# The last stage of a decode step by token tiles, with the residual turned in 32x32 blocks

## The chip, the cores and the metric

One core of a Trainium2 chip runs the whole program in one launch. The metric is the device time of an execution in microseconds. TensorE (PE) multiplies, VectorE (DVE), ScalarE (ACT) and GpSimd (POOL) work elementwise, and SyncE (SP) issues nearly all DMA transfers, in the order of its own queue.

## The reference

A decoder layer for 1024 prompt tokens and 32 sample tokens of width 1024 (1056 rows in all). Two token mixers, retention and latent attention, work on the same normalised input; their outputs are merged, projected and added to the input. The last stage, which the change touches, is

```python
x = x + merged @ w_out
x = x + sigmoid(x @ w_ple_gate) * (ple @ w_ple_proj)
y = rmsnorm(x, final_norm_w)
```

`w_out` and `w_ple_gate` are 1024x1024, `w_ple_proj` is 256x1024, and `ple` has 256 columns per token. The outputs of the stage are `y_prompt` (1024 rows) and `y_sample` (32 rows).

## The kernel before

Products are made from float32 values in two parts: `hi`, a copy in the type that TensorE multiplies at full rate, and `lo`, the rest. `mac` (L262) makes one product from three matmuls, hi by hi, hi by lo and lo by hi (L266 to L268). `gemm` (L270) keeps 128 output features in the partitions and the tokens in the columns, in three thirds of `TH` = 352 columns; for each third it adds up `nk` blocks of 128 in a bank of PSUM (`mm`, two banks) and calls an eviction. `load_w` (L253) brings a strip of 128 weight columns in two loads (`stage`, L240, with `wr` tiles of 256 KB from SP, two rooms), ScalarE copies `hi`, VectorE subtracts `lo`.

The `w_out` stage (L1549 to L1570) runs over eight strips f. Its eviction adds the transposed input `xT` on VectorE, copies `hi` on ScalarE and subtracts `lo` on VectorE: the new residual stands transposed, features in the partitions, as eight pairs `x1h`, `x1l`. In its course the projection's weights (`wph`, `wpl`) and the first third of the embedding (`pT`) are loaded and split.

The gate stage is `third(j, pT)` (L1573), three times. For each strip f it loads 128 columns of `w_ple_gate` (anew in each third), multiplies projection (`pp`, 2 blocks) and gate (`pg`, 8 blocks) with features in the partitions, and then adds `x1h` and `x1l` to `xr` on GpSimd (L1614), takes the sigmoid on ScalarE (L1617), and product and sum on VectorE (L1618, L1619). After every second strip, `turn` (L1581) turns the strips before back to tokens: six transposes on TensorE (L1588, with the identity), squares with their sums on ScalarE (L1590), and the product with the norm's weights on VectorE (L1596). Behind the fourth turn of a third come the root on GpSimd (L1595), the scaling on ScalarE and VectorE (L1627, L1628) and the output.

Rooms in SBUF are shared by tags: `xs_` has 23 rooms of 4.2 KB per partition, of which `merged` holds 16 until `w_out` is done, `w4` three, `xr_` 17. Which instruction comes next on each engine isn't written out by hand in this stage: the framework puts them in an order when it builds the program, and waits follow from the tiles that are read and written. Earlier in the program `turn_blocks` (L329) already writes tokens as features to DRAM by VectorE's 32x32 transposes and DMAs of 32-element pieces, for the latents (`latD`) and the embedding (`pTD`, L333).

Of the kernel before, what the change touches and what calls it, by code (L numbers as in the profile page):

```python
# [20 lines left out]
P = 128  # L21
# [135 lines left out]
def run(g):  # L157
    for _ in g:
        pass
# [3 lines left out]
def decode_step(ctx: ExitStack, tc: tile.TileContext, A: dict, O: dict):  # L163
# [35 lines left out]
    def lo_of(out, src, hi):  # L199
        dve.tensor_tensor(out=out, in0=src, in1=b32(hi), op=ALU.subtract)  # L200
# [20 lines left out]
    latD = dram.tile([NLAT // 32, 32, SEQ], F32, tag="latD", name="latD")  # L221
    xTD = dram.tile([P, 8, NT], F32, tag="xTD", name="xTD")
    pTD = dram.tile([PLE // 32, 32, NT], F32, tag="pTD", name="pTD")

    w_in = A["w_in"][0]

# [26 lines left out]
    def load_w(src, nk):  # L253

        hi, lo = wtiles()
        src = src.rearrange("(k p) f -> p k f", p=P)
        for k in range(0, nk, 4):
            ks = slice(k, min(k + 4, nk))
            stage(src[:, ks], hi[:, ks], lo[:, ks])
        return hi, lo  # L260
# [923 lines left out]
    def split(raw, hi, lo):  # L1184
        act.copy(hi, raw)  # L1185
        lo_of(lo, raw, hi)
        return hi, lo
# [342 lines left out]
        gx = nxt  # L1530


    def by_tile(j):

        for a in range(0, TH, P):
            b = min(a + P, TH)
            yield a, b, min(b, SEQ - j * TH) - a

    def embedding(j):
        pT = [xs_("pT", (P, 2, TH)) for _ in range(2)]  # L1540
        for k in range(2):
            hi, lo = (pT[k][:, i, :] for i in range(2))
            raw = xs_("pTr", (P, TH), F32)
            sp.dma_start(raw, pTD[4 * k:4 * k + 4, :, j * TH:(j + 1) * TH].rearrange("b i t -> (b i) t"))
            split(raw, hi, lo)
        return pT

    x1, wp = [], []
    for f in range(8):  # L1549
        fs = slice(f * P, (f + 1) * P)  # L1550
        xT = nxt_xT
        w = load_w(A["w_out"][0, :, fs], 8)
        hi, lo = xr_("x1h"), xr_("x1l")
        x1.append((hi, lo))

        def evac(j, ps, sl, hi=hi, lo=lo, xT=xT):
            t = wst.tile([P, TH], F32, tag="gev", name="x1", bufs=2)
            dve.tensor_tensor(out=t, in0=ps, in1=xT[:, sl], op=ALU.add)
            act.copy(hi[:, sl], t)
            lo_of(lo[:, sl], t, hi[:, sl])  # L1560
        if f < 7:
            nxt_xT = x_transposed(f + 1)
        run(gemm(w, merged, evac, 8))
        if f in (3, 4):
            k = f - 3
            wp.append(tuple(xs_(n_, (P, D)) for n_ in ("wph", "wpl")))
            for c in (slice(0, 512), slice(512, D)):
                stage(A["w_ple_proj"][0, k * P:(k + 1) * P, c], wp[k][0][:, c], wp[k][1][:, c])
        if f == 6:
            pT = embedding(0)  # L1570


    def third(j, pT):  # L1573
        sl = slice(j * TH, (j + 1) * TH)
        tiles = list(by_tile(j))
        Y = [xs_("yn", (P, D), F32) for _ in tiles]
        ss = small(pz, "ss", 12, 2)
        pool.memset(ss, 1.0)
        r = small(pz, "r", 3, 2)

        def turn(yT, quarter):  # L1581

            hs = slice(quarter * 256, (quarter + 1) * 256)
            for i, ((a, b, _), yn) in enumerate(zip(tiles, Y)):
                n = b - a
                px = tr()
                for c in range(2):
                    pe.transpose(px[:n, c * P:(c + 1) * P], yT[:, c, a:b], ident)  # L1588
                q = xs_("sq", (P, 256), F32)
                act.activation(q[:n], px[:n, :256], AF.Square, accum_out=ss[:n, 4 * i + quarter:4 * i + quarter + 1])  # L1590
                if quarter == 3:
                    v, of = (small(pz, name, 4 if name == "of" else 1, 2) for name in ("v", "of"))
                    dve.tensor_tensor_reduce(out=of, in0=ss[:, 4 * i:4 * i + 4], in1=fours, scale=1.0 / D, scalar=EPS,
                                             op0=ALU.mult, op1=ALU.add, accum_out=v)
                    pool.tensor_tensor(out=r[:, i:i + 1], in0=v, in1=nhalf, op=ALU.pow)  # L1595
                dve.tensor_tensor(out=yn[:n, hs], in0=px[:n, :256], in1=fnw[:n, hs], op=ALU.mult)  # L1596

        due = None
        for f in range(8):
            fs = slice(f * P, (f + 1) * P)  # L1600
            if f % 2 == 0:
                yT = xs_("yT", (P, 2, TH), F32)
            w = load_w(A["w_ple_gate"][0, :, fs], 8)
            pp = ac()
            for k in range(2):
                mac(pp[:, :TH], tuple(v[:, fs] for v in wp[k]), (pT[k][:, 0, :], pT[k][:, 1, :]), k == 0, k == 1)
            pg = mm()
            for k in range(8):
                mac(pg[:, :TH], (w[0][:, k, :], w[1][:, k, :]), (x1[k][0][:, sl], x1[k][1][:, sl]), k == 0, k == 7)
            if f % 2 == 0 and f:  # L1610
                turn(due, f // 2 - 1)
            y = yT[:, f % 2, :]
            xr = xs_("xr", (P, TH), F32)
            pool.tensor_tensor(out=xr, in0=b32(x1[f][0][:, sl]), in1=b32(x1[f][1][:, sl]), op=ALU.add)  # L1614
            sg = wst.tile([P, TH], F32, tag="gev", name="sg", bufs=2)
            for a, b in [(a, b) for a, b, _ in tiles] if f == 7 and j == 2 else [(0, TH)]:
                act.activation(sg[:, a:b], pg[:, a:b], AF.Sigmoid)  # L1617
                dve.tensor_tensor(out=sg[:, a:b], in0=sg[:, a:b], in1=pp[:, a:b], op=ALU.mult)  # L1618
                dve.tensor_tensor(out=y[:, a:b], in0=sg[:, a:b], in1=xr[:, a:b], op=ALU.add)  # L1619
            due = yT  # L1620
            yield
        turn(due, 3)
        for i in range(3):
            (a, b, m), yn = tiles[i], Y[i]
            n = b - a
            o = xs_("o", (P, D), F32)
            act.activation(o[:n, :448], yn[:n, :448], AF.Copy, scale=r[:n, i:i + 1])  # L1627
            dve.tensor_scalar(o[:n, 448:], yn[:n, 448:], r[:n, i:i + 1], None, op0=ALU.mult)  # L1628
            t0 = j * TH + a
            sp.dma_start(O["y_prompt"][0, t0:t0 + m, :], o[:m])  # L1630
            if m < n:
                sp.dma_start(O["y_sample"].rearrange("b t d -> (b t) d"), o[m:n])

    fours = pz.tile([P, 4], F32, name="fours")
    pool.memset(fours, 1.0)
    fnw = w4("fnw", (P, D), F32)
    sp.dma_start(fnw, A["final_norm_w"].unsqueeze(0).to_broadcast([P, D]))
    last = iter(())
    for j in range(3):
        u = third(j, pT)  # L1640
        next(u)
        run(last)
        for f in range(7):
            next(u)
            if f == 4 and j < 2:
                pT = embedding(j + 1)
        last = u
    run(last)
    rph.close()
    ph.close()  # L1650

# [32 lines left out]
```

## Time and profile before

| | |
|---|---|
| median of 3 runs | 2132.06 us (2128.3 to 2132.3) |
| the profiled execution's own time | 2129.97 us |
| its span | 2128.2 us |
| PE busy | 2091.2 us, 98% |
| DVE busy | 1261.7 us, 59% |
| ACT busy | 723.2 us, 34% |
| POOL busy | 333.1 us, 16% |
| DMA over the span | 316.31 MB, 149 GB/s |

The span runs from the first to the last instruction of the program in the profile; 1.8 us of the execution lie around it. Matmuls overlap each other in the records, so the step from one start to the next tells more than the length of one.

### The profile page before, as it was taken

To read this page: it belongs to the slowest core of one execution; us is meant where nothing else is said; L and a number is where in the kernel's file an instruction comes from. 1 tells how busy PE (TensorE), PEld (TensorE's weight loads), DVE (VectorE), ACT (ScalarE), POOL (GpSimd) and SP (SyncE) were. 2 spreads that over 40 slices of the span, in tenths; PEclk is the share of its full clock that TensorE was granted. 3 is DMA by queue.
4 is the path that set the end of the run, shared out by engine and by line. 5 is a ranking of instruction groups with operands and counts; after the bars stand their busy time and mean duration, and the time that the engine had idled before them with its cause. 6 is when DMAs were issued, how large, how long until landed. Compare 5 with 4: busy or idle time off the path is not lost. (4 is left out here: it accounts for less than half of the span.)

```text
span 2128.2 us, 38977 instructions
## 1 busy us (share of the span) xinstructions
PE 2091.2 (98%) x15408; PEld 1835.8 (86%) x15408; DVE 1261.7 (59%) x2850; ACT 723.2 (34%) x1543; POOL 333.1 (16%) x527
## 2 busy tenths in 40 slices
PE   8999999999999999999999999999999999999998
PEld 7998787787877998888888887888888999999997
DVE  6524556565565357677677764877776353444465
ACT  6312232342423322222222212454565341322343
POOL 2220111111110022222222220122211000000122
PEclk9999999999999999999999999999999999999999
DMA  7576666566564322745626647210112452333243
GB/s 208 133 245 212 236 212 225 219 219 239 201 231 169 121 66 75 240 126 152 209 73 195 177 159 242 48 43 23 35 55 89 140 192 82 100 90 119 84 143 118
DMA packets 330552, 316.31 MB, mean 149 GB/s; under 512 B 92160, under 2 KB 283840, under 8 KB 326272
## 3 DMA queue, kind: packets, MB, share of 16 engines
q1 hardware_dynamic: 303872, 208.28, 33.2%
q0 software_dynamic: 9216, 83.89, 10.6%
q10 hardware_dynamic: 17280, 21.63, 2.8%
q8 instruction: 121, 1.98, 0.4%
q14 instruction: 63, 0.52, 0.1%
HBM read 245.38 MB, written 68.36 MB: 147 GB/s over the span
## 5 line engine op out<-in xcount | busy, mean ns | idle before, releaser
L266 PE MATMUL mm<-xh,wh 128*128 128x352 f32 x1344 | 456.5, 340 | 2.1 <-POOL wh L197 1.6
L268 PE MATMUL mm<-xh,wl 128*128 128x352 f32 x1344 | 436.4, 325 | 2.1 <-DVE wl L200 2.1
L267 PE MATMUL mm<-xl,wh 128*128 128x352 f32 x1344 | 436.5, 325 | 0.0
L266 PEld LDWEIGHTS mm<-xh,wh 128*128 128x128 f32 x1344 | 253.1, 188 | 85.7 <-issue 74.7
L268 PEld LDWEIGHTS mm<-xh,wl 128*128 128x128 f32 x1344 | 254.1, 189 | 4.0 <-DVE wl L200 2.4
L267 PEld LDWEIGHTS mm<-xl,wh 128*128 128x128 f32 x1344 | 254.2, 189 | 3.2 <-issue 2.1
L200 DVE TENSOR_TENSOR wl<-wr,wh 128x512 fp32r<-128x512 f32 (+2 forms) x251 | 176.0, 714 | 128.2 <-ACT wh L247 92.2
L247 ACT CAST wh<-wr 128x512 fp32r<-128x512 f32 x214 | 128.4, 618 | 279.0 <-PE mm L267 247.3
L687 DVE STREAM_TRANSPOSE kt<-craw 128x512 f32<-128x512 f32 x256 | 161.1, 681 | 86.9 <-PE sc L691 80.6
L439 ACT ACTIVATE gev<-mm 128x352 f32<-128x352 f32 x120 | 55.5, 463 | 242.1 <-PE mm L268 230.7
L266 PE MATMUL mm<-mh,wh 128*128 128x352 f32 x384 | 124.5, 324 | 1.4 <-ACT mh L1185 0.8
L267 PE MATMUL mm<-ml,wh 128*128 128x352 f32 x384 | 124.8, 325 | 0.8 <-DVE ml L200 0.6
L268 PE MATMUL mm<-mh,wl 128*128 128x352 f32 x384 | 124.3, 324 | 0.0
L268 PE MATMUL mm<-gh,wl 128*128 128x352 f32 x384 | 124.3, 324 | 0.0
L266 PE MATMUL mm<-gh,wh 128*128 128x352 f32 x384 | 124.3, 324 | 0.0
L267 PE MATMUL mm<-gl,wh 128*128 128x352 f32 x384 | 124.1, 323 | 0.0
L266 PE MATMUL mm<-wv,xh 128*128 128x512 f32 x256 | 103.6, 405 | 0.0
L267 PE MATMUL mm<-wv,xh 128*128 128x512 f32 x256 | 100.9, 394 | 0.0
L268 PE MATMUL mm<-wv,xl 128*128 128x512 f32 x256 | 100.8, 394 | 0.0
L691 PE MATMUL sc<-kt,q 32*32 32x512 f32 x2560 | 91.7, 600 | 0.0
L1614 POOL TENSOR_TENSOR xr<-x1h,x1l 128x352 f32<-128x352 f32 x24 | 26.6, 1131 | 389.0 <-DVE pT L200 311.0
L890 ACT ACTIVATE on<-ac,gb,gs 128x512 f32<-128x512 f32 x36 | 28.0, 778 | 157.9 <-DVE gb L888 152.8
(395 smaller groups left out, 4512.2 us busy)
## 6 DMA issues: line engine op xcount, KB each, us to landing
wr<-in_w_in_dram SPq DMA_DIRECT2D x144, 256.0 KB, 3.8
st<-in_state_ret_dram SPq DMA_DIRECT2D x32, 512.0 KB, 4.7
out_ret_sample_dram<-st SPq DMA_DIRECT2D x32, 512.0 KB, 3.6
wr<-in_w_ple_gate_dram SPq DMA_DIRECT2D x48, 256.0 KB, 2.8
gt<-gev ACTq DMA_DIRECT2D x48, 176.0 KB, 3.7
gl<-go SPq DMA_DIRECT2D x16, 528.0 KB, 5.6
gate<-ga SPq DMA_DIRECT2D x16, 528.0 KB, 3.6
g<-gt SPq DMA_DIRECT2D x32, 256.0 KB, 3.2
```

The source lines that it names most:

```text
L200: dve.tensor_tensor(out=out, in0=src, in1=b32(hi), op=ALU.subtract)
L247: hi_by[0](hi, raw)
L266: pe.matmul(out, wh, xh, start=first, stop=False)
L267: pe.matmul(out, wh, xl, start=False, stop=False)
L268: pe.matmul(out, wl, xh, start=False, stop=last)
L439: act.activation(t, ps, func)
L687: dve.transpose(kt[:, 2 * i + s].rearrange("p (n r) -> p n r", r=32), src)
L691: pe.matmul(sc[32 * v:32 * v + 32, q, :], Q["q4"][qs_, j + v // 2, 2 * (g % 2) + v % 2, :], kt[qs_, v, :], start=n == 0, stop=n == NJ // 2 ...
L890: act.activation(on[:n], po, AF.Identity, bias=nb[:n], scale=s[:n])
L1614: pool.tensor_tensor(out=xr, in0=b32(x1[f][0][:, sl]), in1=b32(x1[f][1][:, sl]), op=ALU.add)
```

## The change

The residual is turned to tokens as soon as it is made. Each eviction of `w_out` also transposes its 128x352 piece in 32x32 blocks on VectorE and writes it with four DMAs of 128-byte pieces to a DRAM tensor `x1D` with one row per token. From there `residual(T)` reads 128 tokens at a time.

Gate and projection products come out by tokens: the tokens' `x1h`, `x1l` (or the embedding's parts) are the stationary side and 512 columns of weights, a half H of the features, the moving one. The weights of a half are loaded and split once, 12 tiles of `xs_` and the `wh`, `wl` rooms; half 0 during `w_out`, half 1 during the first four token tiles. The order of the work is token tiles 0 to 3 in half 0, the same in half 1, then both halves of tiles 4 to 7; the last unit comes in two column halves. `joined` takes sigmoid, product, sum and square by tokens, `normed` the root and the scaling.

The 32 sample tokens leave these products. They are computed in plain float32 from unsplit weights (loaded once more, in 20 pieces of 256 KB), with the 32 tokens as the stationary side and four groups of 128 weight columns side by side in the array's column groups, two pieces behind each unit. A small product with a matrix of ones adds the four groups' squares.

`w_out`'s strips are loaded one pass ahead in the code. The GpSimd sums `xr` and the TensorE transposes fall away.

```diff
@@ -221,6 +221,7 @@
     latD = dram.tile([NLAT // 32, 32, SEQ], F32, tag="latD", name="latD")
     xTD = dram.tile([P, 8, NT], F32, tag="xTD", name="xTD")
     pTD = dram.tile([PLE // 32, 32, NT], F32, tag="pTD", name="pTD")
+    x1D = dram.tile([NT, D], F32, tag="x1D", name="x1D")
 
     w_in = A["w_in"][0]
 
@@ -1530,122 +1531,217 @@
         gx = nxt
 
 
...
+    HF = D // 2
+    x1, W, WP = [], {}, {}
+
+    def raw_weight(name, H, k):
+        raw = xs_("raw", (P, 2, HF), F32)
+        for s in range(2):
+            sp.dma_start(raw[:, s], A[name][0, (k + s) * P:(k + s + 1) * P, H * HF:(H + 1) * HF])
+        return raw
+
+    def split_weight(to, H, k, raw, rooms=None):
+        if rooms is None:
+            rooms = tuple(xs_("w", (P, 2, HF)) for _ in range(2))
+        else:
+            rooms = tuple(v.rearrange("p k d -> p (k d)").rearrange("p (s d) -> p s d", s=2) for v in rooms)
+        for s in range(2):
+            hi, lo = to[H, k + s] = tuple(v[:, s] for v in rooms)
+            act.copy(hi, raw[:, s])
+            lo_of(lo, raw[:, s], hi)
+
+    def gate_weight(H, k, rooms=None):
+        split_weight(W, H, k, raw_weight("w_ple_gate", H, k), rooms)
+
+    def tokens(T):
+        return slice(T * P, (T + 1) * P)
+
+    def residual(T):
+        X1[T] = xs_("xy", (P, D), F32)
+        sp.dma_start(X1[T], x1D[tokens(T), :])
+
+    def embedding(u, of):
+        rooms = tuple(of("pT", (P, 2, HF)) for _ in range(2))
+        hi, lo = rooms
         for k in range(2):
...
+            sp.dma_start(b32(lo[:, k]), pTD[4 * k:4 * k + 4, :, u * HF:(u + 1) * HF].rearrange("b i t -> (b i) t"))
+        act.copy(hi, b32(lo))
+        lo_of(lo, b32(lo), hi)
+        for T in range(4):
+            PT[4 * u + T] = tuple(v[:, :, T * P:(T + 1) * P] for v in rooms)
+
+    X1, PT, SS, pgs, pps = {}, {}, {}, {}, {}
+    turned_ = xr_("x1t", (P, 3, TH), F32)
+    nxt_w = load_w(A["w_out"][0, :, :P], 8)
     for f in range(8):
...
+        w, xT = nxt_w, nxt_xT
         hi, lo = xr_("x1h"), xr_("x1l")
         x1.append((hi, lo))
 
...
+        def evac(j, ps, sl, f=f, hi=hi, lo=lo, xT=xT):
             t = wst.tile([P, TH], F32, tag="gev", name="x1", bufs=2)
             dve.tensor_tensor(out=t, in0=ps, in1=xT[:, sl], op=ALU.add)
             act.copy(hi[:, sl], t)
             lo_of(lo[:, sl], t, hi[:, sl])
+            dve.transpose(turned_[:, j].rearrange("p (b r) -> p b r", r=32), t.rearrange("p (b r) -> p b r", r=32))
+            for a in range(0, P, 32):
+                sp.dma_start(x1D[sl, f * P + a:f * P + a + 32].rearrange("(b i) r -> i b r", i=32),
+                             turned_[a:a + 32, j].rearrange("p (b r) -> p b r", r=32))
         if f < 7:
+            nxt_w = load_w(A["w_out"][0, :, (f + 1) * P:(f + 2) * P], 8)
             nxt_xT = x_transposed(f + 1)
+        else:
+            gate_weight(0, 6, wtiles())
+            embedding(0, w4)
+            raw_proj = raw_weight("w_ple_proj", 0, 0)
+        if f % 2 == 0 and f < 6:
+            gate_weight(0, f)
         run(gemm(w, merged, evac, 8))
...
+
+
+    def gate_products(T, H, cols=slice(0, HF)):
+        n = cols.stop - cols.start
+        ps = pgs[T, H, cols.start] = mm()
+        for k in range(8):
+            mac(ps[:, :n], tuple(v[:, tokens(T)] for v in x1[k]), tuple(v[:, cols] for v in W[H, k]), k == 0, k == 7)
+
+    def proj_products(T, H):
+        ps = pps[T, H] = ac()
+        for k in range(2):
+            mac(ps, tuple(v[:, k] for v in PT[T]), WP[H, k], k == 0, k == 1)
+
+    def joined(T, H, cols=slice(0, HF)):
+        n = cols.stop - cols.start
+        if T not in SS:
+            SS[T] = small(pz, "ss", 4, 4)
+            pool.memset(SS[T], 0.0)
+        at_ = slice(H * HF + cols.start, H * HF + cols.stop)
+        y = X1[T][:, at_]
+        sg = gates[:, (2 * T + H) % 2, :n]
+        act.activation(sg, pgs[T, H, cols.start][:, :n], AF.Sigmoid)
+        dve.tensor_tensor(out=sg, in0=sg, in1=pps[T, H][:, cols], op=ALU.mult)
+        dve.tensor_tensor(out=y, in0=sg, in1=y, op=ALU.add)
+        i = 2 * H + (cols.start > 0)
+        act.activation(sg, y, AF.Square, accum_out=SS[T][:, i:i + 1])
+        if T == 7:
+            dve.tensor_tensor(out=y, in0=y, in1=fnw[:, at_], op=ALU.mult)
+
+    def root(ss, n):
+        v, of, r = small(pz, "v", 1, 2), small(pz, "of", 4, 2), small(pz, "r", 1, 2)
+        dve.tensor_tensor_reduce(out=of[:, :n], in0=ss, in1=fours[:, :n], scale=1.0 / D, scalar=EPS, op0=ALU.mult, op1=ALU.add, accum_out=v)
+        pool.tensor_tensor(out=r, in0=v, in1=nhalf, op=ALU.pow)
+        return r
+
+    def normed(T):
+        y, r = X1.pop(T), root(SS.pop(T), 4)
+        if T < 7:
+            dve.scalar_tensor_tensor(out=y, in0=y, scalar=r, in1=fnw, op0=ALU.mult, op1=ALU.mult)
+        else:
+            act.activation(y[:, :448], y[:, :448], AF.Copy, scale=r)
+            dve.tensor_scalar(y[:, 448:], y[:, 448:], r, None, op0=ALU.mult)
+        sp.dma_start(O["y_prompt"][0, tokens(T), :], y)
 
     fours = pz.tile([P, 4], F32, name="fours")
     pool.memset(fours, 1.0)
     fnw = w4("fnw", (P, D), F32)
+    Y = {}
+
+    def sample_rooms():
+        room = xs_("xyS", (P, 2, HF), F32)
...
+        for r in range(4):
+            cs, rs = (slice(r * P, (r + 1) * P), slice(r * NR, (r + 1) * NR))
+            sp.dma_start(Y["x"][rs], x1D[SEQ:, :].rearrange("t (h d) -> t h d", h=2)[:, :, cs])
+            sp.dma_start(Y["w"][rs], A["final_norm_w"].rearrange("(h d) -> h d", h=2)[:, cs].unsqueeze(0).to_broadcast([NR, 2, P]))
+        for k in range(2):
+            sp.dma_start(Y["p"][:, k], pTD[4 * k:4 * k + 4, :, SEQ:].rearrange("b i t -> (b i) t"))
+        for k in range(8):
+            pool.tensor_tensor(out=Y["in"][:, k], in0=b32(x1[k][0][:, SEQ:]), in1=b32(x1[k][1][:, SEQ:]), op=ALU.add)
+        dve.tensor_reduce(out=one, in_=ident.rearrange("p (q r) -> p r q", q=4), axis=AX.X, op=ALU.add)
+        dve.tensor_copy(Y["same"].rearrange("p (q r) -> p q r", q=4), one.unsqueeze(1).to_broadcast([P, 4, NR]))
+        Y["g"], Y["o"] = tr(), tr()
+
+    pieces = [(H, name, k) for H in range(2) for name, n in (("o", 2), ("g", 8)) for k in range(n)]
+    raws = []
+
+    def sample_load():
+        if len(raws) < len(pieces):
+            H, name, k = pieces[len(raws)]
+            src = A["w_ple_gate" if name == "g" else "w_ple_proj"][0, k * P:(k + 1) * P, H * HF:(H + 1) * HF]
+            raw = wst.tile([P, 512], F32, tag="wr", name="wr", bufs=2)
+            sp.dma_start(raw, src)
+            raws.append(raw)
+
+    def sample_products(i):
+        H, name, k = pieces[i]
+        x = (Y["in"] if name == "g" else Y["p"])[:, k]
+        for r in range(4):
+            pe.matmul(Y[name][r * NR:(r + 1) * NR, H * P:(H + 1) * P], x, raws[i][:, r * P:(r + 1) * P], start=k == 0,
+                      stop=k == (7 if name == "g" else 1), tile_position=(0, r * NR), skip_group_check=True)
+        sample_load()
+
+    def sample_sum():
+        w = slice(0, 2 * P)
+        sg, x = Y["in"].rearrange("p k r -> p (k r)"), Y["x"].rearrange("p h c -> p (h c)")
+        act.activation(sg, Y["g"][:, w], AF.Sigmoid)
+        dve.tensor_tensor(out=sg, in0=sg, in1=Y["o"][:, w], op=ALU.mult)
+        dve.tensor_tensor(out=x, in0=sg, in1=x, op=ALU.add)
+        ss = small(pz, "ss", 4, 4)
+        pool.memset(ss, 0.0)
+        act.activation(sg, x, AF.Square, accum_out=ss[:, 0:1])
+        return ss
+
+    def sample_end(ss):
+        total = tr()[:, :4]
+        pe.matmul(total, Y["same"], ss, start=True, stop=True)
+        r = root(total, 4)
+        dve.scalar_tensor_tensor(out=Y["x"], in0=Y["x"], scalar=r, in1=Y["w"], op0=ALU.mult, op1=ALU.mult)
+        for q in range(4):
+            sp.dma_start(O["y_sample"].rearrange("b t (h d) -> (b t) h d", h=2)[:, :, q * P:(q + 1) * P], Y["x"][q * NR:(q + 1) * NR])
+
+    split_weight(WP, 0, 0, raw_proj)
+    gates = xs_("sg", (P, 2, HF), F32)
+    for T in range(2):
+        residual(T)
+        gate_products(T, 0)
+    for T in range(4):
+        if T < 2:
+            residual(T + 2)
+        proj_products(T, 0)
+        joined(T, 0)
+        if T < 2:
+            gate_products(T + 2, 0)
+        if T == 3:
+            split_weight(WP, 1, 0, raw_weight("w_ple_proj", 1, 0))
+        gate_weight(1, 2 * T, wtiles() if T == 3 else None)
     sp.dma_start(fnw, A["final_norm_w"].unsqueeze(0).to_broadcast([P, D]))
...
+    sample_rooms()
+    for i in range(2):
+        sample_load()
+    units = [(T, 1) for T in range(4)] + [(T, H) for T in range(4, 8) for H in range(2)]
+    for n, (T, H) in enumerate(units):
+        if n == 1:
+            embedding(1, xs_)
+        if H and T + 2 in (4, 5, 6, 7):
+            residual(T + 2)
+        proj_products(T, H)
+        for cols in (slice(0, 256), slice(256, 512)) if n == 11 else (slice(0, HF),):
+            gate_products(T, H, cols)
+            joined(T, H, cols)
+        if n < 10:
+            for i in range(2):
+                sample_products(2 * n + i)
+        if H:
+            normed(T)
+        if n == 9:
+            total = sample_sum()
+        if n == 10:
+            sample_end(total)
     rph.close()
     ph.close()
```

## Rows read from the trace of the kernel before

**Rows 1.** The page: engines' busy time and share, ScalarE's weight copies (busy, mean ns).
```profile
PE 2091.2 (98%) x15408; PEld 1835.8 (86%) x15408; DVE 1261.7 (59%) x2850; ACT 723.2 (34%) x1543; POOL 333.1 (16%) x527
...
L247 ACT CAST wh<-wr 128x512 fp32r<-128x512 f32 x214 | 128.4, 618 | 279.0 <-PE mm L267 247.3
```

**Rows 2.** Chain of waits from 1850 us on, shares by line.
```profile
by line: PE mm L268 28.4%; PE mm L266 28.4%; PE mm L267 28.3%; PE ac L267 2.8%; PE ac L268 2.8%; PE ac L266 2.8%; PE tr L1588 2.7%; POOLq L1665 0.6%; POOL r L1595 0.4%; ACT o L1627 0.2%; ACT sq L1590 0.2%; issue 0.1%; DVE sg L1618 0.1%; DVE
```

**Rows 3.** Stretches: length, busy us (instructions) per engine, PEclk, DMA share, GB/s.
```profile
100.00:106.00 6.00, 3.54 (x26) 2.94 (x24) 3.35 (x10) 0.47 (x2) 2.46 (x5) 1.00 0.10 16
106.00:113.00 7.00, 5.75 (x20) 5.75 (x21) 3.18 (x5) 0.00 (x0) 1.69 (x2) 0.51 0.56 118
52.00:60.00 8.00, 8.00 (x56) 7.96 (x55) 2.83 (x8) 4.45 (x12) 2.54 (x7) 1.00 1.04 263
1600.00:1700.00 100.00, 96.86 (x611) 94.16 (x610) 51.70 (x121) 43.10 (x90) 8.05 (x11) 1.00 0.37 122
1900.00:1993.20 93.20, 93.20 (x579) 93.20 (x578) 39.57 (x71) 23.38 (x46) 3.13 (x4) 1.00 0.34 102
1993.30:2117.00 123.70, 123.70 (x789) 123.44 (x788) 74.76 (x149) 52.64 (x146) 27.20 (x28) 1.00 0.41 123
2117.00:2128.20 11.20, 1.29 (x7) 0.60 (x5) 4.11 (x18) 3.68 (x12) 2.58 (x3) 0.63 0.37 129
```

**Rows 4.** Timeline of TensorE in the gate stage: start, us, engine, line, operation.
```profile
1993.35 0.32 PE L266 MATMUL ac<-pT,wph 128*128 128x352 f32 x1
...
2111.30 0.33 PE L268 MATMUL mm<-x1h,wl 128*128 128x352 f32 x1
...
2112.29 0.32 PE L267 MATMUL ac<-pT,wph 128*128 128x352 f32 x1
...
2116.80 0.33 PE L268 MATMUL mm<-x1h,wl 128*128 128x352 f32 x1
```

**Rows 5.** The retention values' product, 780 to 786 us: durations, first and last start.
```profile
L266 PE MATMUL mm<-wv,xh x8: 392/394/478, 780.2 to 785.1; 128*128 128x512 f32 x8
...
L268 PE MATMUL mm<-wv,xl x8: 389/396/396, 780.7 to 785.6; 128*128 128x512 f32 x8
```

**Rows 6.** Timeline of TensorE at a sample product of the retention.
```profile
1291.29 0.42 PE L1064 MATMUL ac<-wvS,xS 128*32 128x128 f32 x8
1291.65 0.43 PE L267 MATMUL mm<-xl,wh 128*128 128x352 f32 x1
```

**Rows 7.** Timeline of the tail, all engines.
```profile
2119.40 2.70 POOL L1595 TENSOR_TENSOR r<-v,cst 128x1 f32<-128x1 f32 x3 [24.84 <-DVE v L1593]
...
2122.13 0.67 ACT L1627 ACTIVATE o<-yn,r 96x448 f32<-96x448 f32 x1 [0.92 <-POOL r L1595]
...
2123.40 0.78 SPq L1632 DMA_DIRECT2D out_y_sample_dram<-o  x1
```

**Rows 8.** Timeline of ScalarE in the gate stage.
```profile
2008.44 0.38 ACT L1590 ACTIVATE sq<-tr 128x256 f32<-128x256 f32 x1
...
2008.81 0.46 ACT L1617 ACTIVATE sg<-mm 128x352 f32<-128x352 f32 x1
2009.15 0.38 ACT L1590 ACTIVATE sq<-tr 128x256 f32<-128x256 f32 x1
```

**Rows 9.** VectorE's groups by shape over the span: busy, mean ns, idle before.
```profile
L200 DVE TENSOR_TENSOR wl<-wr,wh 128x512 fp32r<-128x512 f32 x224 | 163.0, 741 | 118.6 <-ACT wh L247 92.2 <-POOL wh L197 22.0 <-PE mm L563 3.7
...
L1558 DVE TENSOR_TENSOR x<-mm,xT 128x352 f32<-128x352 f32 x24 | 12.6, 524 | 40.6 <-PE mm L268 40.6
...
L846 DVE STREAM_TRANSPOSE kb<-k 128x352 f32<-128x352 f32 x16 | 7.8, 524 | 11.1 <-POOL k L840 11.1
```

**Rows 10.** The embedding's block-wise writes, 1340 to 1400 us: SP's time each (min/median/max).
```profile
L333 SPq DMA_DIRECT2D pTD<-tp x33: 303/448/1016, 1342.7 to 1399.4; - x33
```

**Rows 11.** DMA queue, 1372.8 to 1377 us: packets, MB, share of 16 engines.
```profile
q1 hardware_dynamic: 1232, 0.26, 30.5%
```

**Rows 12.** The latents' block-wise writes, 44 to 60 us: SP's time each.
```profile
L333 SPq DMA_DIRECT2D latD<-lt x4: 420/1010/1212, 54.9 to 57.8; - x4
```

More of the change, by code (lines that the diff above doesn't have):

```diff
@@ L1530, in decode_step @@
         gx = nxt
[L1533 to L1540, printed above, removed]
-        for k in range(2):
[L1542 to L1546, printed above, removed]
@@ L1548, in decode_step @@
-    x1, wp = [], []
+    HF = D // 2
[14 more added lines that the diff above has]
+            lo_of(lo, raw[:, s], hi)
@@ L1549, in decode_step @@
+    X1, PT, SS, pgs, pps = {}, {}, {}, {}, {}
+    turned_ = xr_("x1t", (P, 3, TH), F32)
+    nxt_w = load_w(A["w_out"][0, :, :P], 8)
     for f in range(8):
-        fs = slice(f * P, (f + 1) * P)
-        xT = nxt_xT
-        w = load_w(A["w_out"][0, :, fs], 8)
+        w, xT = nxt_w, nxt_xT
         hi, lo = xr_("x1h"), xr_("x1l")
         x1.append((hi, lo))
-        def evac(j, ps, sl, hi=hi, lo=lo, xT=xT):
+        def evac(j, ps, sl, f=f, hi=hi, lo=lo, xT=xT):
             t = wst.tile([P, TH], F32, tag="gev", name="x1", bufs=2)
@@ L1564, in decode_step @@
[L1564 to L1632, printed above, removed]
@@ L1636, in decode_step @@
     fnw = w4("fnw", (P, D), F32)
-    sp.dma_start(fnw, A["final_norm_w"].unsqueeze(0).to_broadcast([P, D]))
[L1638 to L1648, printed above, removed]
+    Y = {}
+    def sample_rooms():
+        room = xs_("xyS", (P, 2, HF), F32)
+        Y["x"] = room[:, 0, :256].rearrange("p (h c) -> p h c", h=2)
+        Y["w"] = room[:, 0, 256:512].rearrange("p (h c) -> p h c", h=2)
+        Y["in"] = room[:, 1, :256].rearrange("p (k r) -> p k r", k=8)
+        Y["p"] = room[:, 1, 256:320].rearrange("p (k r) -> p k r", k=2)
+        Y["same"] = room[:, 1, 320:448]
+        one = room[:, 1, 448:480]
+        for r in range(4):
[9 more added lines that the diff above has]
+        Y["g"], Y["o"] = tr(), tr()
```

## The prediction

> **What bounds the kernel now.** The page comes first: TensorE is busy for 98% of the span [rows 1]. A busy share alone proves little where matmuls overlap, so the chain of waits of the stretch that the change touches is next, from 1850 us on. There the matmuls L266 to L268 make up 85% of the chain, the projection's matmuls ("ac") 8.4% and the transposes L1588 2.7%; nothing else reaches 1% [rows 2]. The table by stage says the same: TensorE has no idle time while `w_out` is multiplied (1900 to 1993 us) nor in the gate stage (1993.3 to 2117), at full clock, with VectorE at 74.8 and ScalarE at 52.6 of 123.7 us; then comes a tail of 11.2 us almost without TensorE [rows 3]. So the end moves with three things: the matmul time of the last stage, the holes that open in it, and the tail.
>
> **The gate stage's matmuls.** Before: 3 thirds x 8 strips x (2 + 8) k x 3 parts = 720 matmuls of 352 columns, and 12 turns of 6 transposes. The first starts at 1993.35, the last at 2116.80: 123.45 us. From the last matmul ahead of a turn (2111.30) to the second behind it (2112.29) lie 0.99 us in place of two ordinary steps of 0.16, so a turn costs 0.67 us [rows 4]; eleven turns lie ahead of the last matmul, 7.4 us. The rest, 116.1 us over 719 steps, is 161 ns per 352 columns, 0.459 ns per column.
>
> After: 8 token tiles x 2 halves x 10 k x 3 parts = 480 matmuls of 512 columns (the last unit is cut in two column halves, same columns). The retention values are such a product already, tokens as the stationary side and 512 weight columns moving: 24 matmuls, the first starting at 780.2 and the last at 785.6, 5.4 us over 23 steps, 235 ns [rows 5]; 512 times 0.459 is 235 too. 480 x 0.235 = 112.8 us. I take that; 232 or 238 would move it by 1.4 us.
>
> The samples' 32 columns leave these products and come as 20 groups of four 32-column matmuls with float32 weights. Eight of that shape (two groups) occupy TensorE for 0.36 us, from 1291.29 to the next matmul at 1291.65 [rows 6]: 10 x 0.36 = 3.6 us, and 0.3 for the small product that adds up their squares. The transposes go. Sum 116.7 in place of 123.45: **6.8 us less**.
>
> **The tail.** Before: after the last matmul (2116.80) come sigmoid, product and sum by tiles, six transposes, three roots on GpSimd one after another (2.70 us for three), three scalings, the last ending at 2122.8, and the last of four output DMAs issued at 2123.40, 6.6 us behind the last matmul [rows 7]. After: one tile and its last 256 columns. 0.4 for the matmul itself and the handover; sigmoid, product, sum and square of 256 columns at about 0.4 each (a square of 256 took 0.38 [rows 8]) and 0.2 to read its sum, 1.8 together; the sum over four columns 0.25; one root at 0.9 (2.70 / 3); a scaling at 0.67 [rows 7]: 4.0 us, so the issue comes 2.6 us earlier. Its transfer is 512 KB and not 128 KB; I give back 0.5. **2.1 us less**, between 1 and 3.
>
> **What `w_out`'s stage gets on top.** Every eviction gains a 32x32-block transpose of 128x352 on VectorE (0.52 us [rows 9]) and four DMAs; in every other pass 512 KB of gate weights are split. VectorE per pass of 11.65 us (93.2 / 8): 3 x (0.52 + 0.52 + 0.52) for sum, split and transpose and 2 to 4 splits of weights at 0.74 [rows 9] is 6.2 to 7.6 us. It fits, and the matmul banks are freed by the first operation of an eviction, ahead of the new one. I cost it at nothing; without that cover a late eviction would stop TensorE, since two banks hold two thirds.
>
> SP issues 16 DMAs per pass (12 of the turned residual, 2 of `w_out`, 1 of the transposed input, 1 of gate weights on average) in place of 3. The nearest row is the block-wise write of the embedding, whose issue took 0.45 us at the median, 0.30 to 1.02 [rows 10]: 16 x 0.45 = 7.2 of 11.65 us. Weights queued behind them are wanted a pass later. The packets: 96 DMAs x 32 rows x 11 blocks = 33,792 of 128 bytes. Four embedding writes (1024 such packets) and a load of 128 KB took 30.5% of 16 engines over 4.2 us [rows 11], 1.28 us; if all of that were the small packets, the residual costs 42 us of 93, 45%. That comes on top of the 34% which the stage has [rows 3] and of six more weight loads of 256 KB (the gate stage's 41% of 123.7 us over its 48 loads is 1.06 us each at most, 7% here). That is 0.86 at most, so the transfers stay under what the engines carry. Below nothing it can't go: TensorE has no idle time to win there.
>
> The Trainium skill ("DMA: Bandwidth & Descriptors", section "Specifications") speaks against this part: below 512 bytes the DMA engines read, modify and write, so line rate is lost. If that doubled the packets' time, they would take 84 of 93 us and the stage, with 41% of other transfers, would be overfull; by it the rival "SP and DMA" below holds and the time is some 2139 us, by the row above it is hidden.
>
> **The joints.** Two new places have no cover in the trace of before, so I bound them. (1) From `w_out` to the first gate products: they need the last strip's split and weights of the last pass, both early; the residual is read back from DRAM, some 9 us after the last matmul (eviction 1.5, four issues 2, landing 2, load 3.5), and wanted after two gate units and a projection, 48 x 0.235 + 1.4 = 12.7 us. GpSimd's 24 sums fall away in turn. (2) From half 0 to half 1: six weight pairs are split within 120 steps, 28.2 us, where ScalarE has 6 x 2 x 0.62 [rows 1] for copies and 4 x 1.4 for the units, 13 us, and VectorE 6 x 2 x 0.74 and 4 x 1.4, 14.5 us. Both fit if the copies run as soon as their loads land. The nearest joint in the trace, from attention to the first output projection, lost 3.1 us of TensorE in 100 [rows 3]; the joint from `w_out` to the gates of before lost nothing. Each joint costs 0 to 3.1; I take 1 each, **2.0 us more**, nearer to the joint of before, as that has the same kinds of load. Later units (7.0 us and two sample groups each) leave ScalarE and VectorE some 2 us of work per unit; residuals and sample weights come a unit or more ahead.
>
> Sum: -6.8 - 2.1 + 2.0 = **-6.9 us**. The profiled execution took 2129.97 us: 2123.1. (The median of the runs is 2.1 us above it; I stay on the profiled one.) What a measurement of this kernel tells from no change is about 0.2%, 4.3 us.
>
> **Rivals.**
>
> *No change: a hole at the change of halves.* If ScalarE and VectorE run in written order, the second projection weights wait behind the units: after the fourth unit's gate products come a projection 1.4, then product and sum 1.4, square 0.8, two copies 1.2, sigmoid 0.6, product and sum 1.4, square 0.8, two copies 1.2, a split 0.7, 9.5 us in all, while TensorE has 2.8 us of projections. It stands 6.7 us. At 104 to 107 us TensorE stood for some 3.7 us in two waits, and was at half clock (0.51) from 106 to 113 [rows 3]; work worth 3.4 us was lost that way, and would be here. -8.9 + 6.7 + 3.4 = +1.2: 2131 us. For it: the code's order. Against: the trace doesn't keep that order. At 2008.81 ScalarE computed the sigmoid of a strip that stands behind three squares in the code, after the first of them [rows 8]; what was ready went first.
>
> *Slower: SP and DMA in `w_out`'s stage.* Where the DMA engines were full (52 to 60 us, share 1.04 [rows 3]), block-wise writes of the latents took SP 1.01 us each at the median [rows 12]. The rival decides from 11.65 / 16 = 0.73 us per issue: above it SP falls behind in each pass and `w_out`'s weights come late. At 0.85 a pass lasts 13.6 us, 8 x 2.0 = 16 more: -6.9 + 16 = +9, 2139 us. For it: 33,792 packets where that stage had none. Against: the share stays at or under 0.86, and the embedding's writes beside full weight traffic took 0.45.
>
> *More than I say.* No holes at all and the short end of the tail: -6.8 - 3 = 2120 us. That is the lower end of the forecast rather than a case of its own.
>
> **Chances.** Forecast 0.68, with its own range 2119.5 to 2127.5 (rate 1.4, tail 1, joints -2 to +4). Hole at the halves 0.17, SP and DMA 0.12, 0.03 for holes in the sample part, a few us either side of no change. Range 2118.5 to 2131.5: it holds the forecast and the hole, and leaves out the slower case and a little on each side. Faster by over 0.2% (under 2125.7): 0.95 of the forecast, 0.65. Same: the rest of the forecast, most of the hole's and the last 0.03, 0.20. Slower: SP and DMA and a hole longer than worked out, 0.15.
>
> **What would show it.** Right: 512-column steps at 235 ns; TensorE without idle time from the first `w_out` pass to the end of the gate stage, but for a us or two at the two joints; DMA share 0.6 to 0.85 in `w_out`'s stage and x1D issues at 0.45 us; last matmul to the end of the span 9.3 us in place of 11.4. Wrong: waits of a `w_out` product for its weights behind SP (the slower rival); the second half's first projection waiting for VectorE's split, with PEclk falling behind it (the hole); column steps over 240 ns.

## The result: 2140.8 us, slower by half a per cent

The changed kernel takes 2140.84 us (median of 6, 2137.8 to 2146.7), the kernel before beside it 2131.43 us: a ratio of 1.0049, 95% interval 1.0036 to 1.0061. The forecast was 2123.1 us, with a range up to 2131.5. The profiled execution took 2137.81 us, its span is 2136.0 us, 7.8 us longer than before. By stage:

| stage | before | after | difference |
|---|---|---|---|
| up to the first `w_out` matmul | 1900.23 | 1898.79 | -1.4 |
| `w_out` stage | 93.1 | 107.3 | +14.2 |
| gate stage, first to last matmul | 123.45 | 120.38 | -3.1 |
| from there to the end of the span | 11.4 | 9.54 | -1.9 |

The table by stage of the kernel after, to be read beside [rows 3] (length; busy us and instructions of PE, PEld, DVE, ACT, POOL; granted clock; DMA share; GB/s). The first line is passes 0 to 2 of `w_out`, the second passes 3 to 7, then gate stage and tail:

```profile
1898.79:1933.70 34.91, 34.91 (x217) 34.91 (x217) 18.54 (x35) 8.87 (x17) 0.00 (x0) 1.00 0.53 117
1933.70:2006.10 72.40, 63.67 (x362) 60.75 (x361) 28.73 (x55) 11.99 (x24) 0.00 (x0) 0.95 0.50 115
2006.10:2126.40 120.30, 119.87 (x667) 94.02 (x666) 47.20 (x81) 31.05 (x68) 7.26 (x21) 1.00 0.45 148
2126.40:2136.00 9.60, 0.37 (x4) 0.17 (x2) 1.87 (x6) 1.56 (x4) 0.55 (x1) 0.72 0.14 55
```

The first three passes run as before, 11.64 us each. Then they take 14.77, 15.82, 13.90, 15.83 and 12.09 us. In the second line the whole loss can be read: 72.40 - 63.67 = 8.7 us in which TensorE has no work, and 63.67 us busy for 360 matmuls that take 58.2 at 0.1616 each, 5.5 us of slower work (3.4 of it at half clock, as told below). TensorE's waits from 1890 us on (us in total, times, longest) name what it stood for:

```profile
PE mm L267 <- ACT wh L248: 6.6, 4, 1.7
PE mm L269 <- DVE wl L200: 1.8, 5, 0.6
PE tr L1684 <- DMA wr<-in_w_ple_gate_dram: 0.3, 1, 0.3
PE mm L267 <- DVE x L1583: 0.3, 1, 0.3
```

The first matmul of a pass waits for ScalarE's copy of the strip's upper half (L248; L247 before), the third for VectorE's lower half. Why they are late is seen on ScalarE's timeline and on the tile `wr` (instructions: ns min/median/max, first and last start) around the change of strip at 1946.8:

```profile
1943.62 0.48 ACT L1584 CAST x1h<-x 128x352 fp32r<-128x352 f32 x1 [3.07 <-DVE x L1583]
1947.42 0.48 ACT L1584 CAST x1h<-x 128x352 fp32r<-128x352 f32 x1 [3.32 <-DVE x L1583]
1947.81 1.14 ACT L248 CAST wh<-wr 128x512 fp32r<-128x512 f32 x2
```

```profile
L247 SPq DMA_DIRECT2D wr<-in_w_out_dram x2: 412/432/452, 1937.0 to 1937.5; - x2
DMA to landing us min/median/max: 2.8/3.1/3.3
```

The strip was loaded by 1940.8 (issued at 1937.5, 3.3 us on the way), and ScalarE sat idle for 3.07 us around and behind that moment and for 3.32 us later. Yet the copies stand behind the copy of the eviction that ends the pass (1947.42), directly ahead of their own use. In the kernel before they stood a pass ahead; its ScalarE timeline:

```profile
1946.83 1.14 ACT L247 CAST wh<-wr 128x512 fp32r<-128x512 f32 x2
...
1958.46 1.14 ACT L247 CAST wh<-wr 128x512 fp32r<-128x512 f32 x2 [2.67 <-PE mm L267]
```

There a pair of copies ran at the start of a pass, as soon as the last use of its room was over (a matmul of L267 at the end of the pass before), and served the pass that began 11.6 us later. So in ScalarE's order of instructions the copies slipped by one pass.

At two of the four changes of strip with that wait, at 1946.8 and 1976.5, the clock falls as well, 3 and 4 us after the stop began:

```profile
1949.69:1953.10 3.41, 3.41 (x12) 3.41 (x13) 0.40 (x1) 0.00 (x0) 0.00 (x0) 0.50 0.42 65
1980.42:1983.90 3.48, 3.48 (x14) 3.48 (x13) 0.00 (x0) 0.00 (x0) 0.00 (x0) 0.51 0.80 192
```

3.4 us at 0.50 of full speed, the 1.2 GHz level: 1.7 us of work lost each time.

### The profile page after: what moved, and what is told of

It reads as the page before. It is cut to its first block, busy times and chain, and to the rows that moved or that the text cites. A ratio compares the mean times of both kernels' runs of the same rounds, so it can differ in the third digit from the quotient of the medians.

```text
span 2136.0 us, 38639 instructions
## 1 busy us (share of the span) xinstructions
PE 2091.7 (98%) x15282; PEld 1808.1 (85%) x15282; DVE 1242.3 (58%) x2791; ACT 699.2 (33%) x1455; POOL 308.0 (14%) x517
## 5 line engine op out<-in xcount | busy, mean ns | idle before, releaser
L267 PE MATMUL mm<-xh,wh 128*128 128x352 f32 x1344 | 456.1, 339 | 2.0 <-POOL wh L197 1.6
L267 PEld LDWEIGHTS mm<-xh,wh 128*128 128x128 f32 x1344 | 252.9, 188 | 85.4 <-issue 74.5
L200 DVE TENSOR_TENSOR wl<-wr,wh 128x512 fp32r<-128x512 f32 (+2 forms) x203 | 139.2, 700 | 86.8 <-ACT wh L248 55.7
L248 ACT CAST wh<-wr 128x512 fp32r<-128x512 f32 x166 | 99.2, 618 | 210.9 <-PE mm L268 187.1
L267 PE MATMUL mm<-mh,wh 128*128 128x352 f32 x384 | 126.4, 329 | 8.3 <-ACT wh L248 6.6
L267 PE MATMUL mm<-gh,wh 128*128 128x352 f32 x384 | 124.3, 324 | 0.0
L267 PE MATMUL mm<-wv,xh 128*128 128x512 f32 x256 | 103.5, 404 | 0.0
L267 PEld LDWEIGHTS mm<-mh,wh 128*128 128x128 f32 x384 | 73.4, 191 | 10.3 <-ACT wh L248 7.8
```

The costliest lines, as they stand in the source:

```text
L248: hi_by[0](hi, raw)
L267: pe.matmul(out, wh, xh, start=first, stop=False)
```

## The experiments

The theory: what costs is the place of the strips' copies and subtractions in ScalarE's and VectorE's order, and the 96 writes of x1D on SP, the queue of the strips' loads, moved it (why they move it when the program is built, no run looks at). The rivals: the strips' transfers are late by themselves behind those writes; VectorE's transposes hold the change of strip; the writes load the DMA engines. Ratios are to the kernel before in the same session; stages are from the profiles (before 93.1 and 123.45, after 107.3 and 120.38).

### e1: the casts' place fixed by hand

An instruction marked with `keep_in_program_order` keeps, on its engine, the place that it has in the code. The two loads of a strip stay a pass ahead in the code; its copies and subtractions move into the first eviction.

```diff
+            if j == 0 and f < 7:            # casts of the next strip, behind the first eviction
+                for k, raw in enumerate(raws_w): ...
...
-            act.copy(hi[:, sl], t)
+            copied = act.copy(hi[:, sl], t)
+            if j and f < 7:
+                tc.keep_in_program_order(copied)
```

> The changed kernel, but each strip of `w_out` is cast to its upper half behind the first eviction of the pass before it, a place fixed by hand; in the changed kernel it stood behind the third. Transposes, writes of x1D and their queue stay as they are. Theory (place in ScalarE's order): the raw strips had landed 6 us before they were cast, so only the cast's place was late; passes 3 to 6 of the `w_out` stage return from 13.9 to 15.8 us to about 11.7, the stage from 107.3 to 93 to 95 us, the time from 2140.8 to 2125 to 2129. Rival (the weights' transfers are late, behind twelve writes each pass on SP): the transfers are the same, the stage stays over 103 us and the time over 2136. Rival (VectorE's transposes hold the lower halves): the same, over 2136.

Measured: 2136.13 us, ratio 1.0012 [1.0001, 1.0024]; the stage 100.5 us. The time lies at the edge of what the rivals forecast (2136), the stage under theirs (103) and above the theory's: half of the loss is gone. TensorE's waits from 1890 us on, and its timeline at a change of strip:

```profile
PE mm L269 <- DVE wl L200: 4.6, 5, 1.5
```

```profile
1951.14 0.32 PE L268 MATMUL mm<-ml,wh 128*128 128x352 f32 x1
1952.91 0.43 PE L269 MATMUL mm<-mh,wl 128*128 128x352 f32 x1 [1.46 <-DVE wl L200]
```

The wait for ScalarE's copy (6.6 us) is gone, that for VectorE's lower half has grown from 1.8 to 4.6. VectorE's order was left free in this run, and there the eviction that ends the pass stands ahead of the strip:

```profile
1951.18 0.53 DVE L1583 TENSOR_TENSOR x<-mm,xT 128x352 f32<-128x352 f32 x1 [2.70 <-PE mm L269]
1951.74 0.55 DVE L1588 STREAM_TRANSPOSE x1t<-x 128x352 f32<-128x352 f32 x1
1952.21 1.25 DVE L200 TENSOR_TENSOR wl<-wr,wh 128x512 fp32r<-128x512 f32 x2
```

### e5: VectorE's place fixed too

```diff
+            added = dve.tensor_tensor(out=t, in0=ps, in1=xT[:, sl], op=ALU.add)
+            if j and f < 7:
+                tc.keep_in_program_order(added)
```

> The kernel of the run with the casts pinned, and the place of VectorE's additions fixed as well, so that the lower halves of a `w_out` strip (two subtractions of 0.6 us) stand behind the first eviction of the pass before and no longer behind the first of their own. Transposes, writes and SP's queue as in the changed kernel. In that run the casts were on time and TensorE waited up to 1.77 us at a change of strip for the lower halves. Theory (place in the engines' orders, and nothing else): passes 3 to 6 fall from 12.95 and 13.35 us to 11.65, the stage from 100.5 to 93 to 94, the time from 2136.1 to 2127 to 2131. Rival (writes on SP delay the weights themselves): the waits remain in another guise, stage 98 or more, time over 2133.

Measured: 2128.36 us, ratio 0.9977 [0.9968, 0.9987]. The `w_out` stage:

```profile
1905.70:1998.80 93.10, 93.10 (x578) 93.10 (x577) 47.24 (x90) 21.87 (x41) 0.00 (x0) 1.00 0.59 133
```

No idle time, 11.64 us in each pass, full clock, with every transpose and every write on SP as in the changed kernel. Nor do the strips come earlier: ScalarE waits for one of them here, which lands at 1948.06 for the pass that begins at 1952.22, 4.2 us ahead (7.7 us in the changed kernel, 1940.8 for 1948.47), and TensorE waits for nothing in the stage.

```profile
1948.08 0.62 ACT L1597 CAST wh<-wr 128x512 fp32r<-128x512 f32 x1 [0.45 <-DMA wr<-in_w_out_dram]
```

This settles the cause within the kernel: the place in the two engines' orders.

### e2, e3, e10: writes and loads kept apart

e2: `sp.dma_start(x1D...)` becomes `pool.dma_start(x1D...)`. e3: the loop over `a` becomes one write,

```diff
+            sp.dma_start(x1D[(3 * f + j) * 44:(3 * f + j + 1) * 44, :].rearrange("a b -> (a b)")..., turned_[:, j])
```

and e10: `load_w`'s loads in the `w_out` stage become `act.dma_start`.

> The changed kernel with the writes of x1D issued by GpSimd in place of SP, the same 96 writes of the same bytes. Theory: SP's queue has only the loads, the casts stand a pass ahead as in the kernel before, and the stage takes 93 to 95 us, the time 2125 to 2128. Rival (SP's order is innocent, the transposes or the transfers' load on the DMA engines cost the time): 2136 to 2142.

> The changed kernel with one write of x1D for each eviction in place of four: 24 in all, 128 rows of 1408 bytes, where 96 had pieces of 128 bytes. Transposes stay; the residual that the last stage reads has its pieces in the wrong places, so the y outputs are not the reference's, with the same work behind them. Theory (the writes shift the order): the casts stand a pass ahead, the stage takes 93 to 95 us, the time 2124 to 2128. Rival (VectorE's transposes): stage over 103 us, time over 2136. It does not tell the order from the transfers: both would be cured.

> The changed kernel with the raw strips of `w_out` (14 loads) issued by ScalarE in place of SP; the writes stay on SP. Theory (loads and writes on one queue): the loads no longer stand behind writes, the casts stand a pass ahead again, the stage takes 93 to 96 us, the time 2125 to 2130; each load takes a place on ScalarE, 0.5 us or so of its 6 us idle per pass, at no cost. Rival (the writes slow SP or the DMA engines for all loads): stage over 100 us, time over 2135.

Measured: e2 2127.63 us, ratio 0.9967 [0.9953, 0.9980]; e3 2126.13, 0.9962 [0.9949, 0.9975]; e10 2135.26, 0.9967 [0.9954, 0.9979]. The session of e10 ran the kernel before at 2142.26 us, so its time missed the numbers expected while the ratio is that of e2. `w_out` and gate stage of e2:

```profile
1903.80:1996.90 93.10, 93.10 (x577) 93.10 (x577) 50.18 (x94) 23.89 (x46) 52.36 (x85) 1.00 0.55 138
1996.90:2117.90 121.00, 120.05 (x667) 94.18 (x666) 44.11 (x77) 28.23 (x63) 14.49 (x33) 1.00 0.43 143
```

In all three the stage takes 93.1 us. The order, which nobody fixed there, went back to a pass ahead as soon as loads and writes had different queues (e2, e10) or the writes were few (e3); in e2 these copies serve the pass that begins at 1961.99:

```profile
1950.43 1.14 ACT L248 CAST wh<-wr 128x512 fp32r<-128x512 f32 x2 [2.71 <-PE mm L268]
```

The writes took GpSimd 52 us, on an engine with nothing else to do in this stage. Not all that e2 gains is the stage's: from its last matmul to the end of the span it takes 7.95 us, as e8 does, where the changed kernel takes 9.54, e3 and e10 9.55. Most of these 1.6 us lie at the very end, behind SP's last entry; the cause was not looked for.

### e4: the transposes taken away

```diff
+    pool.memset(turned_, 0.0)
...
-            dve.transpose(turned_[:, j]..., t...)
+            dve.tensor_copy(turned_[:, j]...[:, :, :1], t...[:, :, :1])
```

> The changed kernel with each of the 24 transposes by VectorE replaced by a copy of one column in 32 (0.1 us or so where the transpose takes some 0.5), so that the residual of the last stage is not the reference's; writes and their queue stay. Theory (place in ScalarE's order, shifted by the writes): the casts stay late, the time stays at 2136 to 2141. Rival (VectorE's added 1.5 us per pass hold the boundary): the stage falls by 10 us or more, the time to 2124 to 2129.

Measured: 2138.36 us, ratio 1.0020 [1.0006, 1.0034]. The time is as the theory has it, the stage is 102.3 us and not 107.3; the stage, and TensorE's waits from 1890 us on:

```profile
1907.30:2009.70 102.40, 95.23 (x579) 92.70 (x578) 39.09 (x90) 20.85 (x41) 0.00 (x0) 1.00 0.53 122
```

```profile
PE mm L267 <- ACT wh L248: 6.6, 4, 1.7
```

The wait for the copies stands to the tenth, the one for `wl` is gone, and the clock did not fall (1.00). The transposes don't cause the slip; in these profiles it is dearer with them, by 1.8 us of waits and two falls of the clock.

### e7, e9: the kernel before, with the writes alone

Transposes and writes of the change added to the eviction of the kernel before, whose last stage stays; e7 issues the writes by SP, e9 by GpSimd.

> The kernel before, with the change's transposes by VectorE and its 96 writes of x1D on SP added to the `w_out` stage and nothing else; nobody reads what they write. Theory (the writes shift the loads and casts of the strips behind the evictions): several passes grow by 2 to 4 us, the stage from 93.1 to 101 to 108, the time 8 to 14 us above the kernel before. Rival (the loss needs the new last stage's loads, those of the gate's weights beside the writes): the stage stays under 95, the time within 3 us of the kernel before.

> The kernel before with the same transposes and 96 writes of x1D as in the run that took 2163.7 us, the writes issued by GpSimd in place of SP. There the chain of waits went from an eviction through its transpose and its four writes on SP to a load of `w_out` queued behind them, 2.8 to 4.2 us on the way, and so to its cast. Theory (what costs is the place of the loads behind the writes on one queue, in the plan and in the queue): the passes are 11.64 us again, the `w_out` stage 93 to 94 us, the time within 3 us of the kernel before. Rival (transposes, or the bytes and pieces of the writes, on the DMA engines): the stage stays above 100 us, the time over 2140.

Measured: e7 2163.73 us, ratio 1.0147 [1.0130, 1.0165], 31 us of loss and over twice what was expected; e9 2144.88 us beside 2142.26, ratio 1.0016 [1.0006, 1.0025]. The two stages of e7, TensorE's waits from 1900 us on, and the chain of waits at a change of strip:

```profile
1903.60:2021.50 117.90, 98.54 (x579) 97.51 (x578) 50.05 (x92) 23.03 (x44) 3.29 (x4) 0.90 0.46 102
2021.50:2154.30 132.80, 126.57 (x787) 125.83 (x787) 77.20 (x152) 55.20 (x148) 27.44 (x28) 0.96 0.43 128
```

```profile
PE mm L267 <- ACT wh L248: 25.6, 3, 12.7
```

```profile
1938.71 0.54 DVE x L1560
...
1939.27 0.56 DVE x1t L1563
...
1939.84 0.30 SPq L1565
...
1941.77 2.80 DMA wr<-in_w_out_dram
...
1944.67 0.63 ACT wh L248
...
1945.34 0.66 PE mm L267
```

Two of the three waits lie in the `w_out` stage (6.7 and 12.7 us); the third, 6.2 us, stands at the first strip of the gate stage, loaded behind the last writes; that stage takes 9.3 us longer than before. Here it isn't the copy's place but the load itself: it stands on SP behind the four writes of the eviction that ends the pass, is issued at 1941.7 and is wanted at once. So the rival of the late transfer, which fell for the changed kernel, is right for this one. With the writes on GpSimd the stage of e9 is back:

```profile
1910.00:2003.10 93.10, 93.10 (x578) 93.10 (x577) 48.95 (x93) 23.48 (x46) 53.48 (x87) 1.00 0.59 143
2003.10:2132.80 129.70, 126.83 (x787) 126.04 (x787) 80.33 (x151) 53.09 (x146) 36.47 (x41) 0.97 0.41 122
```

Its gate stage stays 6 us longer than before in this one profile, with 2.9 us idle and a granted clock of 0.97; that was not followed up.

### e6: the price of the sample products

```diff
-        for r in range(4):
+        for r in range(4 if k == 0 else 0):     # start and stop set for that one
```

> The changed kernel with 16 of the 20 groups of four sample products left out (only the first of each sum is multiplied), their loads kept; the sample output is not the reference's. Reading of the trace after: a group of four takes about 0.36 us of TensorE, so the gate stage falls by 16 x 0.36 = 5.8 us, from 120.3 to 114 to 115, the `w_out` stage stays at 102 to 107, the time falls by about 6 to 2133 to 2136. The price in the prediction (0.36 for two groups, 0.18 each): the stage falls by 2.9 us to 117.4, the time to 2138. Rival (the groups hide in other waits): no change.

Measured: 2134.71 us, ratio 1.0011 [0.9999, 1.0022]; `w_out` stage 107.3 us. Its gate stage:

```profile
2014.60:2128.50 113.90, 113.75 (x539) 91.55 (x538) 47.10 (x81) 31.11 (x68) 7.27 (x21) 1.00 0.48 156
```

120.38 - 113.99 = 6.4 us for 16 groups (first to last matmul), 0.40 each (some of the 1 us of waits at the first groups may have gone with them). The price in the prediction was half of that.

### e8: what the samples need first, first

The two `pTD` loads of `sample_rooms` go ahead on SP, the eight of residual and norm weights to GpSimd, on top of e2.

> The run with the writes issued by GpSimd, and the two loads of the samples' embeddings, which the first sample product needs, ahead on SP, while the eight loads of their residual and norm weights, needed only at the end, are issued by GpSimd. In that run TensorE lost about 1.5 us at the first two groups of sample products to these loads. Theory (they wait behind eight DMAs of 0.6 us each on SP): the hole goes, the gate stage falls from 121.0 to 119.3 to 119.6, the time from 2127.6 to 2126, 0.25 to 0.4% under the kernel before. Rival (the loads of the sample weights are what is late, 4 us each): the hole stays, 2127 to 2128.

Measured: 2124.20 us, ratio 0.9968 [0.9956, 0.9981]. TensorE has no wait left in either stage:

```profile
1902.00:1995.10 93.10, 93.10 (x578) 93.10 (x577) 50.20 (x94) 23.89 (x46) 52.40 (x85) 1.00 0.56 138
1995.10:2114.30 119.20, 119.20 (x666) 94.44 (x665) 44.13 (x77) 28.24 (x63) 18.64 (x41) 1.00 0.44 145
```

The hole is gone, 1.8 us by the profile; the ratio can't be told from e2's. By the ratios it is faster than both kernels, 0.32% under the one before.

## Why the prediction was wrong, point by point

**"What `w_out`'s stage gets on top ... I cost it at nothing": the step that failed.** It cost 14.2 us, twice the gain forecast elsewhere. The working was a sum of busy times: VectorE, SP and the transfers all fit into 11.65 us, and they did: 47.3 us of VectorE in 107.3, writes on SP at 0.46 us each, DMA share 0.51.

```profile
L1588 SPq DMA_DIRECT2D x1D<-x1t x89: 302/463/1387, 1905.0 to 2005.9; - x89
```

What the sum left out is order. "Weights queued behind them are wanted a pass later" held only while the copies stood a pass ahead, and that distance lies in the order that the framework gives each engine when the program is built: a copy whose strip was there did not run while ScalarE idled. e5 shows that with the copies and subtractions kept ahead of their pass the step does cost nothing.

**The rival "SP and DMA" named the right outcome by the wrong mechanism.** Its 2139 us came out by luck, its sign ("`w_out`'s weights come late") only for the copies and not for the loads. It decides "from 11.65 / 16 = 0.73 us per issue", and the issues took 0.46, against 0.45 forecast from [rows 10]. SP wasn't behind: from 1880 us on it stood 42.2 us waiting for transposed pieces to write. The argument against the other rival, that "what was ready went first", holds the same mistake: it took an order that had been planned for one that the chip makes. At 1944 us the strip was there, ScalarE was idle, and it did not go first (e1 shows that nothing else held it).

**The small packets.** What the Trainium skill says in "DMA: Bandwidth & Descriptors", section "Specifications" (below 512 bytes the engines read, modify and write), was weighed as a doubling of their time. Queue 1 went from 33.7% of 93.2 us (the share 0.34 in [rows 3]) to 50.4% of 107.3, 31 to 54 us of the 16 engines:

```profile
q1 hardware_dynamic: 39913, 12.32, 50.4%
```

That is 23 us more; as the other transfers of the stage carried 1.1 MB less than before, the writes' own part is rather 26 (an estimate, at the 31 us for 9.37 MB of before). Both are under the 42 taken as a ceiling and far from 84, and no wait of TensorE in the `w_out` stage of e5 or e10, which have the same writes, comes from it. The DMA share of the whole stage was 0.51, and 0.59 in e5, where 0.6 to 0.85 had been named.

**The columns: right.** From 2075.14 to 2080.46 lie 23 steps of 512 columns, 0.231 us each, where [rows 5] gave 0.235; 480 steps are 111.0 us in place of 112.8.

```profile
2075.14 0.40 PE L267 MATMUL mm<-w,x1h 128*128 128x512 f32 x1
...
2080.46 0.40 PE L269 MATMUL mm<-wh,x1l 128*128 128x512 f32 x1
2080.78 0.65 PE L1684 MATMUL tr<-wr,xyS 128*32 128x128 f32 x16
2081.36 0.50 PE L267 MATMUL ac<-w,pT 128*128 128x512 f32 x1
```

**The samples: mis-sized by half.** "Eight of that shape (two groups)": a float32 matmul leaves two records, so the x8 in [rows 6] was one group of four. The trace after has 160 records for 80 matmuls, 16 in a unit:

```profile
L1684 PE MATMUL tr<-wr,xyS x160: 269/273/297, 2044.6 to 2112.1; 128*32 128x128 f32 x160
```

In the fence above, two groups take 0.58 us from start to next start, 0.1 more on either side of them, some 0.8 per unit where 0.36 was put down. In e8, which has no holes, all that isn't 512-column steps comes to 119.3 - 111.0 = 8.3 us, against 3.9 forecast. Halving a shape's price by miscounting its records cost 4.4 us.

**The joints: 1.0 us, not 2.0.** From `w_out` to the gates no time was lost (2005.96 to 2006.12). The change of halves made no hole either, so that rival is out. What was lost (120.38 - 119.34 of e8) lay at the first sample products, behind loads on SP.

**The tail: 9.54 us, 9.3 forecast.** The rows that answer to [rows 7], from the last matmul on:

```profile
2126.50 0.27 PE L269 MATMUL mm<-wh,x1l 128*128 128x256 f32 x1
2126.87 0.38 ACT L1621 ACTIVATE sg<-mm 128x256 f32<-128x256 f32 x1 [0.99 <-PE mm L269]
...
2129.39 0.55 POOL L1632 TENSOR_TENSOR r<-v,cst 128x1 f32<-128x1 f32 x1 [8.86 <-DVE v L1631]
2129.97 0.67 ACT L1640 ACTIVATE xy<-xy,r 128x448 f32<-128x448 f32 x1 [1.26 <-POOL r L1632]
...
2130.66 0.35 SPq L1642 DMA_DIRECT2D out_y_prompt_dram<-xy  x1
```

The issue comes 4.2 us after the last matmul (4.0 forecast). One root took 0.55 and not 0.9; the product with the norm's weights between square and root had been left out.

With `w_out`'s stage at 93.1 the forecast would have held within its own range: gate stage -3.1 and tail -1.9 make -5 us in place of -6.9, as the samples' 4.4 and the tail's 0.2 us too little were partly made up by 1.8 us in the columns and 1.0 in the joints. And e5, the change with only its orders fixed, is 0.23% under the kernel before.

## What to carry to other kernels

Work that fits into every engine's idle time can still cost more than the change gains if it moves other work in an order that is fixed when the program is built: ask not only whether an engine has room, but which instruction a preload stands behind. In this kernel the bulk writes that hang on evictions belonged on another queue than the loads of the next operands: moving them was worth more than the whole change. Where records are counted as instructions, check the count against the code before a price is made of it.

## What the runs showed of the hardware

The clock did not fall at every stop, nor at the same stop each time. In the kernel after, each of four changes of strip has a stop of 1.8 us for the upper half and a second one right behind it for the lower. After two of them, whose second stop took 0.64 us, the granted clock went to 0.50 (the 1.2 GHz level); after the two with 0.32 us it stayed at 1.00. The stage of e6 has the same stops, and there the clock fell after the first of them (second stop 0.64 us) and the last (0.32), and not after the other two:

```profile
1958.35:1961.76 3.41, 3.41 (x13) 3.41 (x12) 0.23 (x1) 0.00 (x0) 0.00 (x0) 0.50 0.40 59
2002.72:2006.13 3.41, 3.41 (x14) 3.41 (x13) 0.00 (x0) 0.00 (x0) 0.00 (x0) 0.50 0.76 163
```

So the second stop's length alone does not decide; what does, these runs don't show. Each of these falls lasted 3.4 us. In e4, with the same first stops and second ones of 0.3 us or none, the clock stayed at 1.00.

The profiled start of the `w_out` stage lies between 1898.8 and 1910.0 us over these twelve kernels, though the products up to there are the same, while the stage itself is 93.1 us in each of those that don't wait in it. A stage's length in the trace tells tenths of a us where the whole time tells only about 4.

The 128-byte writes, 96 in 33,792 pieces, cost TensorE nothing in e5, 93.1 of 93.1 us busy. The transfers beside them did not all stay as fast: the loads of `xT` (528 KB) took 5.3 us to land at the median, 3.6 in the kernel before; those of `w_out` took 3.1, and 3.7 before.
